# Moving the shared expert, the row buffers, the excess loop and the final additions of a mixture-of-experts kernel

## The chip, the cores and the metric

The kernel runs on 1 core of one Trainium2 chip. The metric is the device time of one execution in microseconds (us); lower is better. The median of the runs of the kernel before is 2158.79 us.

## The reference, cut to what matters

Two layers run one after the other. Each has a token mixer (attention and a gated spatial branch) and then a mixture of experts; the change lies in the second part alone. There are 512 tokens of width 1024 (`D`), 64 experts with an inner width of 256, and each token goes to 8 of them; one more expert, the shared one, sees every token.

```python
def run_block(args):
    e, toks, ws = args
    xb = x_pad[toks]
    hb = jax.nn.silu(xb @ w_gate[e]) * (xb @ w_up[e])
    return (hb @ w_down[e]) * ws[:, None]

yb = lax.map(run_block, (blk_expert, tok_buf.reshape(n_blocks, MOE_BLOCK), w_buf.reshape(n_blocks, MOE_BLOCK)))
routed = jax.ops.segment_sum(yb.reshape(P, D), tok_buf, num_segments=T + 1)[:T]
shared = (jax.nn.silu(xt @ ws_gate) * (xt @ ws_up)) @ ws_down
return (routed + shared).reshape(B, S, D)
```

The layer then adds this to `ALPHA * x` and normalises; the last layer also multiplies by a gain and adds a bias (`ln2_g`, `ln2_b`).

## The kernel before, in words

**Units.** `moe` sorts the experts by their number of tokens, at run time. The sorted experts have fixed capacities (`CAPS`), and these are cut into 43 units of 128 rows, u0 to u42; some hold part of a large expert, others two to four small ones. Which sorted expert lies in which unit is known when the program is built; only the expert's number is read at run time (`eid`). Each expert's weights are three loads of 1 MB: gate and up columns for one half of the inner sum, the same for the other half, and the down matrix. `load` (L787) issues them on SP.

**Ring of weight slots.** `wnew` hands out slots in turn: six (tag `w`) and three (tag `wd`), and after the routing two more (`w2`). The shared expert's three parts go through the same slots, and each is held until the last piece that reads it.

**One unit on PE.** `gate_up` (L800) runs half 0, then the h of the unit before is transposed (`turn`, L813), then `gate_up` half 1, and then `down` (L826) of the unit before. `scatter` (L1042, POOL) writes the unit's rows into the DRAM array `ysl`. Before each even unit PE transposes the token rows of a pair of units ahead (`turn_pair`, L1005), and `bring_pair` (L1021) works out the slots of the next pair and lets POOL gather its rows (L1026). The gathered rows stay in a row buffer until they are transposed.

**The shared expert** is cut into 12 pieces, three for each 128 tokens (half 0, half 1, and turn with down). `drain(side, n)` runs n of them: five while the routing is worked out, four at u0, two at u1 and one at u2. They read `hT`, a 16 KB per partition tile with the tag `L16`. The two row buffers for pairs from the third on (`rowbuf`) take the place of `hT`, so their gathers wait for the last gate and up piece.

**The loop for excess blocks** (`beyond`) serves experts with more rows than their capacity. It is a `For_i` over a count read at run time, in front of u14, with six weight parts already asked for (`AHEAD`). With these inputs the count is zero: the body never runs, but the engines meet at its branch.

**The end of a layer.** The last two units (`LATE = 2`) are not scattered: `late_mark` and `late` make one-hot matrices and split their rows, and L1266 adds them by matmuls. `collect` loads `ysl` back in 16 loads of 1 MB on SP (L1192), which go through the ring too. For each of the four 128-token tiles: eight matmuls of the late rows (L1266), four additions on DVE of half of the loaded slots (L1270), 16 identity matmuls for the other half (L1274), the sum into `x` (L1277), statistics and normalisation. In the last layer `affine` (L1256, L1257) applies `ln2_g` and `ln2_b`, which SP loads behind the 16 loads, into a ring slot.

**POOL's other work** is `stream`: three operations for each tile that fold `ln1_g`, `ln1_b` and the shared expert's rows into `x`; three steps of it run per unit from u3 on.

Of the kernel before, what the change touches and what calls it, by code (L numbers as in the profile page):

```python
# [41 lines left out]

BEYOND = 14
AHEAD = 6
assert len(CAPS) == E
# [129 lines left out]
def trunk(tc, A):  # L175
# [167 lines left out]
    def mixer(l, st):  # L343
# [352 lines left out]
        st["bring"] = bring  # L696
        t = bring.tile([128, 2048], F32, tag="w", bufs=6, name="rw")
        rw, rb = t[:, 0:NK * E].rearrange("p (k e) -> p k e", k=NK), t[:, NK * E:(NK + 1) * E]
# [53 lines left out]
    def moe(l, st):  # L752
# [12 lines left out]

        more = []
        turns = [0]

        def wnew():

            n = turns[0] % (9 + (MORE if more else 0))
            turns[0] += 1
            if n >= 9:
                return more[0].tile([128, 2048], F32, tag="w2", bufs=MORE, name="we")
            if n % 3 == 2:
                return bp.tile([128, 2048], F32, tag="wd", bufs=3, name="wd")
            return bring.tile([128, 2048], F32, tag="w", bufs=6, name="we")
# [61 lines left out]
        def shared():  # L839
            for i in range(NT):  # L840
                ps = psum()
                for half in range(2):
                    gate_up(hT[:, :, i * 128:(i + 1) * 128], SH, half, ps)
                    if half:
                        h = swiglu(ps, 128)
                    yield
                t = turn(h, 128)
                down(t, SH, 128, None, ysh[:, i])
                yield

# [211 lines left out]
        def bring_pair(p):  # L1062
# [4 lines left out]
            for b_, u_ in enumerate(units_of(p)):  # L1067
                G[u_] = slots(P, b_ * 128, UNITS[u_], None, rbuf[p % 2][:, b_])
                if u_ >= n_units - LATE:
                    zero = bp.tile([128, D], F32, tag="y", bufs=3, name="zero")  # L1070
                    gp.memset(zero, 0.0)
                    scatter(zero, G[u_][1])

        def turn_pair(p):
            xg = bp.tile([128, NK, 256], F32, tag="xg", bufs=2, name="xg")
            gather([rbuf[p % 2][:, b_] for b_ in range(len(units_of(p)))], xg)
            for b_, u_ in enumerate(units_of(p)):
# [3 lines left out]
        mark_pair(0)  # L1081
        rbuf[0] = bp.tile([128, 2, D], F32, tag="xg", bufs=2, name="rows")
        bring_pair(0)
        mark_pair(1)
        drain(side, 1)
        rbuf[1] = bp.tile([128, 2, D], F32, tag="xr", bufs=1, name="rows")
        bring_pair(1)
# [34 lines left out]
        off = small([128, 1], "off", keep=True)  # L1122
        turn_pair(0)
        got1 = rbuf[1]

        def beyond():

            free = rbuf[BEYOND // 2 % 2]
            nov = nc.values_load(ovr[0:1, 128:129], min_val=0, max_val=128)
# [24 lines left out]
        mark_pair(2)  # L1154
        more.append(ch)

        def stream():
            gp.tensor_scalar(lnr, lnr, ALPHA, None, op0=OP.mult)  # L1158
            for i in range(NT):
                gp.tensor_tensor(x[:, i], x[:, i], lnr[:, 0], op=OP.mult)  # L1160
                yield
                gp.tensor_tensor(x[:, i], x[:, i], lnr[:, 1], op=OP.add)
                yield
                gp.tensor_tensor(x[:, i], x[:, i], ysh[:, i], op=OP.add)
                yield

        slow = [stream()]
        lates = []
# [17 lines left out]
        def collect():  # L1186

            for i in range(NT):
                for a in range(TOP // 2):
# [3 lines left out]
                    got.append(t)  # L1193

        got = []
        for u_ in range(n_units + 1):
            if u_ % 2:
                mark_pair(u_ // 2 + 3)
            else:
                if u_ == BEYOND:  # L1200
                    for r, part in [(s[0], part) for u in UNITS[u_:] for part in range(3) for s in u][:AHEAD]:
                        get(r, part)
                    beyond()
                if u_ and units_of(u_ // 2 + 1):
# [3 lines left out]
            if u_ < n_units:  # L1208
                ps = psum()
                xT = G[u_][0]  # L1210
                gate_up(xT, UNITS[u_], 0, ps)
            if u_ >= 1:
# [4 lines left out]
            if u_ == 0:  # L1217
                rbuf[1] = got1
# [7 lines left out]
                gp.dma_start(lnr[:, 0], A["ln1_g"][l:l + 1, :].to_broadcast([128, D]))  # L1226
                gp.dma_start(lnr[:, 1], A["ln1_b"][l:l + 1, :].to_broadcast([128, D]))
            if u_ >= 1:
# [20 lines left out]
        if last:  # L1249
            lnr = bp.tile([128, 2, D], F32, tag="wd", bufs=3, name="lnr")  # L1250
            nc.sync.dma_start(lnr[:, 0], A["ln2_g"][l:l + 1, :].to_broadcast([128, D]))
            nc.sync.dma_start(lnr[:, 1], A["ln2_b"][l:l + 1, :].to_broadcast([128, D]))

        def affine(i):
            for eng, cs in ((dve, slice(0, 640)), (gp, slice(640, 1024))):
                eng.tensor_tensor(x[:, i, cs], x[:, i, cs], lnr[:, 0, cs], op=OP.mult)  # L1256
                eng.tensor_tensor(x[:, i, cs], x[:, i, cs], lnr[:, 1, cs], op=OP.add)  # L1257
            nc.sync.dma_start(A["out"][i * 128:(i + 1) * 128, :], x[:, i])

        for i in range(NT):  # L1260
            mine = got[i * TOP // 2:(i + 1) * TOP // 2]
            fin = [psum() for _ in range(2)]
            for n, (PT, yg) in enumerate(lates):
                for a in range(2):
                    for h in range(2):
                        pe.matmul(fin[h], PT[:, i * 128:(i + 1) * 128], yg[:, a, h * 512:(h + 1) * 512],  # L1266
                                  start=n == 0 and a == 0, stop=False)
            for t in mine[:2]:
                for j in range(2):
                    dve.tensor_tensor(x[:, i], x[:, i], t[:, j], op=OP.add)  # L1270
            for n, t in enumerate(mine[2:]):
# [156 lines left out]
```

## Time and profile before

| | us |
|---|---|
| runs of the kernel | 2158.79, 2152.85, 2159.09 |
| profiled execution | 2155.73 |
| its span in the trace | 2153.9 |
| PE busy | 1973.7 (92%) |
| DVE busy | 996.9 (46%) |
| ACT busy | 500.9 (23%) |
| POOL busy | 370.5 (17%) |

The profiled execution's own time is 1.8 us over its span and 3.1 us under the median. The page's 40 slices alternate between two kinds: the mixers, with little DMA, and the two expert stages (about 380 to 1075 us, and 1425 us to the end), where the 16 DMA engines move 350 to 420 GB/s in most slices while PE is nearly always busy too. A busy share of 92% on PE therefore doesn't tell which of the two sets the time inside an expert stage; the windows of a stage do.

### The profile page before, as it was taken

Reading aid. Unit: us, or ns where it says so; the run is one execution under the profiler, and the core shown is the slowest. Engines: PE = TensorE matmul, PEld = TensorE weight load, DVE = VectorE, ACT = ScalarE, POOL = GpSimd, SP = SyncE. Lnnn points to the kernel's source line nnn. Section 1 sums busy time; section 2 is a strip of 40 time slices with the busy share of each in tenths; the row PEclk is TensorE's granted clock in tenths of the full one; section 3 lists DMA queues with packets and bytes.
Section 4 is the critical chain, followed back from the end, with each engine's and each line's share of the span. In section 5 each row is a group of like instructions: output and inputs, shape, how many; then the busy total and the mean of one; then the engine's idle time right before and its main releaser. Section 6 shows DMA issues by size and latency. Waiting matters only on the chain. (4 is left out here: it accounts for less than half of the span.)

```text
span 2153.9 us, 29150 instructions
## 1 busy us (share of the span) xinstructions
PE 1973.7 (92%) x10820; PEld 1105.5 (51%) x10820; DVE 996.9 (46%) x2065; ACT 500.9 (23%) x1015; POOL 370.5 (17%) x355
## 2 busy tenths in 40 slices
PE   5999999889979999999999999989899799999993
PEld 4867788443334433333477688864433344333341
DVE  6767867523323332321668575753243233332245
ACT  3474232211111111111155533221111111111110
POOL 1101101015411111111130000010361111111113
PEclk9999999899999999999999999989999999999997
DMA  7503665558989999998853144545799899999983
GB/s 277 184 31 134 212 213 186 216 190 355 420 366 407 421 420 402 412 416 373 348 184 108 37 151 165 182 173 204 269 408 415 359 422 420 415 411 415 405 350 157
DMA packets 120128, 626.29 MB, mean 291 GB/s; under 512 B 19472, under 2 KB 19472, under 8 KB 65968
## 3 DMA queue, kind: packets, MB, share of 16 engines
q1 hardware_dynamic: 92912, 550.99, 64.8%
q0 software_dynamic: 27072, 73.42, 9.2%
q8 instruction: 86, 1.41, 0.3%
q14 instruction: 58, 0.48, 0.1%
HBM read 596.02 MB, written 51.38 MB: 301 GB/s over the span
## 5 line engine op out<-in xcount | busy, mean ns | idle before, releaser
L800 PE MATMUL ps<-we,xg 128*32 128x512 f32 (+2 forms) x2544 | 573.0, 597 | 10.2 <-DMA we<-in_w_exp 10.1
L826 PE MATMUL ps<-we,hTt 128*32 128x512 f32 (+2 forms) x1344 | 315.1, 599 | 15.3 <-DMA we<-in_w_exp 11.5
L807 DVE TENSOR_TENSOR h<-h,ps 128x256 f32<-128x256 f32 x94 | 39.6, 421 | 574.0 <-ACT h L805 574.0
L800 PEld LDWEIGHTS ps<-we,xg 128*32 128x32 f32 (+2 forms) x2544 | 171.4, 124 | 254.2 <-issue 210.2
L800 PE MATMUL ps<-wd,xg 128*32 128x512 f32 (+2 forms) x1104 | 286.4, 601 | 3.5 <-DMA wd<-in_w_exp 3.5
L832 DVE SCALAR_TENSOR_TENSOR y<-ps,wc,r 128x512 f32<-128x512 f32 x172 | 129.1, 751 | 197.8 <-PE ps L826 197.8
L1042 POOL DMA_INDIRECT ysl<-y,ii x82 | 85.9, 1047 | 729.0 <-DVE y L832 626.5
L298 PE MATMUL ps<-wH,hH 128*128 128x512 f32 (+1 forms) x512 | 196.2, 383 | 4.2 <-ACT hH L193 4.2
L299 PE MATMUL ps<-wL,hH 128*128 128x512 f32 (+1 forms) x512 | 194.2, 379 | 1.5 <-DVE wL L295 1.5
L300 PE MATMUL ps<-wH,hL 128*128 128x512 f32 (+1 forms) x512 | 194.1, 379 | 0.0
L826 PEld LDWEIGHTS ps<-we,hTt 128*32 128x32 f32 (+2 forms) x1344 | 96.0, 124 | 172.3 <-issue 131.5
L826 PE MATMUL ps<-wd,hTt 128*32 128x512 f32 (+2 forms) x544 | 166.5, 608 | 12.8 <-DMA wd<-in_w_exp 6.8
L1012 ACT ACTIVATE xg<-ps,f 128x256 f32<-128x256 f32 (+1 forms) x176 | 85.4, 556 | 241.4 <-DVE xg L1014 241.4
L193 ACT ACTIVATE hTt<-ps 128x256 f32<-128x256 f32 x94 | 36.0, 383 | 453.5 <-PE ps L813 453.3
L193 ACT ACTIVATE wH<-w 128x1024 fp32r<-128x1024 f32 x83 | 87.6, 1059 | 196.3 <-PE ps L300 110.6
L800 PEld LDWEIGHTS ps<-wd,xg 128*32 128x32 f32 (+2 forms) x1104 | 79.3, 123 | 101.7 <-issue 87.3
L295 DVE TENSOR_TENSOR wL<-w,wH 128x1024 fp32r<-128x1024 f32 x84 | 102.3, 1220 | 50.0 <-ACT wH L193 50.0
L805 ACT ACTIVATE h<-ps 128x256 f32<-128x256 f32 x94 | 36.0, 383 | 357.5 <-PE ps L800 357.5
L1005 PE MATMUL ps<-kc,rowbuf 128*128 128x128 f32 x624 | 83.9, 290 | 37.6 <-DMA we<-in_w_exp 21.9
L1026 POOL DMA_INDIRECT rowbuf<-xd,it x78 | 79.6, 1021 | 221.8 <-PE ps L800 104.6
L236 DVE SCALAR_TENSOR_TENSOR acc<-wa,cond,acc 128x1024 f32<-128x1024 f32 x80 | 106.5, 1331 | 7.5 <-DMA acc<-in_b_ada 4.0
L298 PEld LDWEIGHTS ps<-wH,hH 128*128 128x128 f32 x512 | 97.5, 190 | 23.2 <-ACT hH L193 5.3
(330 smaller groups left out, 2703.3 us busy)
## 6 DMA issues: line engine op xcount, KB each, us to landing
we<-in_w_exp SPq DMA_DIRECT2D x280, 1024.0 KB, 21.4
wd<-in_w_exp SPq DMA_DIRECT2D x104, 1024.0 KB, 20.9
wa<-in_w_ada SPq DMA_DIRECT2D x96, 512.0 KB, 4.4
w<-in_wA SPq DMA_DIRECT2D x92, 512.0 KB, 4.4
we<-ysl SPq DMA_DIRECT2D x24, 1024.0 KB, 18.0
wd<-ysl SPq DMA_DIRECT2D x8, 1024.0 KB, 17.9
we<-in_w_sh SPq DMA_DIRECT2D x4, 1024.0 KB, 9.8
xd<-x SPq DMA_DIRECT2D x8, 512.0 KB, 4.1
```

The costliest lines, as they stand in the source:

```text
L193: return act.activation(out, in_, AF.Copy)
L236: dve.scalar_tensor_tensor(acc, w, cond[:, k:k + 1], acc, op0=OP.mult, op1=OP.add)
L295: dve.tensor_sub(l_out, src, h_out.bitcast(F32))
L298: pe.matmul(ps, aH, wH, start=first, stop=False)
L299: pe.matmul(ps, aH, wL, start=False, stop=False)
L300: pe.matmul(ps, aL, wH, start=False, stop=last)
L800: pe.matmul(ps[c:c + m, :], xT[:, k, c:c + m], ws[s][:, kk * 512:(kk + 1) * 512], start=k == 0, stop=k == NK - 1)
L826: pe.matmul(ps[c:c + m, :], t[:, j, c:c + m], ws[s][:, j * 1024 + nh * 512:j * 1024 + (nh + 1) * 512], start=j == 0, stop=j == 1)
L832: dve.scalar_tensor_tensor(y[0:n, hs], ps[0:n], wcol[0:n], gate2[0:n, hs], op0=OP.mult, op1=OP.mult)
L1005: pe.transpose(ps[:, kk * 256 + b_ * 128:kk * 256 + (b_ + 1) * 128], r[:, (k2 * 2 + kk) * 128:(k2 * 2 + kk + 1) * 128], ident)
L1012: act.activation(xg[:, k, 0:n], o, AF.Identity, bias=sh2[:, k:k + 1], scale=sc2[:, k:k + 1])
L1042: gp.indirect_dma_start(out=ysl[l], out_offset=IndirectOffsetOnAxis(ap=ii[:, 0:1], axis=0), in_=y, in_offset=None, bounds_check=T * TOP - ...
```

## The change

1. **Own slots for the shared expert.** Its three parts get slots `s`, `s`, `sd`. The experts' ring is `w, w, wd` twice, with the two `w2` eight slots; when the last shared piece is done, `s`, `sd`, `s` join it (eleven).
2. **The 12 pieces** are spread: three in the routing, then one at each unit from u3 to u11 (`SIDE = 3`); the call at u12 ends the generator, which extends the ring, loads `ln1_g` and `ln1_b` (POOL's queue) and starts `stream`.
3. `turn_pair(0)` and u0's half 0 stand between the steps of the routing where two shared pieces stood.
4. **One row buffer** (tag `xr`, two units) in place of two; a pair's rows are transposed before the next pair is gathered.
5. **`beyond()`** stands at u41, behind the last weight loads and ahead of `collect`, without loads ahead of its own.
6. **The additions of tiles 0 and 1** (`add`, L1210) are issued at u42, those of tiles 2 and 3 in their tile as before.
7. `ln2_g` and `ln2_b` are loaded on POOL's queue into the row buffer's place.

PE at the end of the routing, layer 0: `we,hT` are gate and up matmuls of the shared expert, `we,xg` of a unit; L1097 to L1113 are the routing's last steps. Before:

```order
L1021 MATMUL ps<-WT,P 128x196 x8
L800 MATMUL ps<-we,hT 128x512 x4
L1097 MATMUL ps<-ov,kc 64x1
L1098 MATMUL ps<-ones,ov 1x1
L800 MATMUL ps<-we,hT 128x512 x4
L1112 MATMUL ps<-le,ones 1x128
L1113 MATMUL ps<-lt,capb 128x128
L1005 MATMUL ps<-kc,rows 128x128 x16
L800 MATMUL ps<-we,xg 32x512 x16
```

And now (L1028 is the transpose, L1044 the slots):

```order
L1044 MATMUL ps<-WT,P 128x196 x8
L1028 MATMUL ps<-kc,rows 128x128 x16
L1120 MATMUL ps<-ov,kc 64x1
L1121 MATMUL ps<-ones,ov 1x1
L800 MATMUL ps<-we,xg 32x512 x16
L1136 MATMUL ps<-le,ones 1x128
L1137 MATMUL ps<-lt,capb 128x128
L800 MATMUL ps<-wd,xg 32x512 x3
```

The two shared pieces are gone from here, and u0's half 0 stands in the chain, with its second half right behind.

PE near the layer's end, now: u41's second half, u40's down, the loop with its body, then u42.

```order
L800 MATMUL ps<-we,xg 128x512 x4
L826 MATMUL ps<-we,hTt 128x512 x4
L1151 TENSOR_LOAD ovr
L1152 COMPARE_AND_BRANCH
L1152 UNCONDITIONAL_BRANCH x2
...
L1152 UNCONDITIONAL_BRANCH
L800 MATMUL ps<-wd,xg 128x512 x4
L813 MATMUL ps<-kc,h 128x128 x2
L800 MATMUL ps<-we,xg 128x512 x4
L826 MATMUL ps<-we,hTt 128x512 x4
L813 MATMUL ps<-kc,h 128x128 x2
L826 MATMUL ps<-we,hTt 128x512 x4
L1276 MATMUL ps<-yg,PT 128x512 x8
```

The branch, which stood between u13's half 1 with u12's down and u14's half 0, now lies between u40's down and u42's half 0.

DVE at the same place; `ix` and `PT` are the one-hot matrix of a late unit, `y` its rows, `yg` their split. Before:

```order
L295 TENSOR_TENSOR yg<-y,yg 128x512 x2
L1173 TENSOR_SCALAR ix<-tk 128x1
L1174 TENSOR_SCALAR PT<-kc,tk 128x256
L1175 TENSOR_SCALAR PT<-kc,ix 128x256
L832 SCALAR_TENSOR_TENSOR y<-ps,wc,r_2302 128x512 x2
L295 TENSOR_TENSOR yg<-y,yg 128x512 x2
L1270 TENSOR_TENSOR x<-x,we 128x1024 x4
L1277 TENSOR_TENSOR x<-ps,x 128x512 x2
```

And now (with the tiles' numbers, which tell u41's from u42's):

```order
L294 TENSOR_TENSOR yg_8283<-y_8274,yg_8283 128x512 x2
L1210 TENSOR_TENSOR x_69<-x_69,we_8219 128x1024 x2
L1210 TENSOR_TENSOR x_69<-x_69,wd_8221 128x1024 x2
L1210 TENSOR_TENSOR x_69<-x_69,we_8227 128x1024 x2
L1210 TENSOR_TENSOR x_69<-x_69,wd_8229 128x1024 x2
L1185 TENSOR_SCALAR ix_8302<-tk_7745 128x1
L1186 TENSOR_SCALAR PT_8301<-kc_65,tk_7745 128x256
L1187 TENSOR_SCALAR PT_8301<-kc_65,ix_8302 128x256
L832 SCALAR_TENSOR_TENSOR y_8306<-ps_8307,wc_7743,r5_2302 128x512
L294 TENSOR_TENSOR yg_8315<-y_8306,yg_8315 128x512 x2
L1286 TENSOR_TENSOR x_69<-ps_8320,x_69 128x512
```

Eight additions, of tiles 0 and 1, now stand between the split of u41's rows and everything that u42's rows need.

```diff
-BEYOND = 14
-AHEAD = 6
+SIDE = 3
...
-        more = []
+        ring = ["w", "w", "wd"] * 2
         turns = [0]
...
+        from_pool = {"w": (bring, 4), "wd": (bp, 2), "s": (bring, 2), "sd": (bp, 1)}
+
+        def wnew(tag=None):
+
+            if tag is None:
+                tag = ring[turns[0] % len(ring)]
+                turns[0] += 1
+            p, n = from_pool[tag]
+            return p.tile([128, 2048], F32, tag=tag, bufs=n, name="wd" if tag in ("wd", "sd") else "we")
 
         def load(which, part):
-            t = wnew()
+            t = wnew(("s", "s", "sd")[part] if which == "shared" else None)
...
                 down(t, SH, 128, None, ysh[:, i])
+                yield
+
+            ring.extend(["s", "sd", "s"])
+            gp.dma_start(lnr()[:, 0], A["ln1_g"][l:l + 1, :].to_broadcast([128, D]))
+            gp.dma_start(lnr()[:, 1], A["ln1_b"][l:l + 1, :].to_broadcast([128, D]))
+            slow.append(stream())
...
-                G[u_] = slots(P, b_ * 128, UNITS[u_], None, rbuf[p % 2][:, b_])
+                if b_ == 0:
+                    rbuf[p] = bp.tile([128, 2, D], F32, tag="xr" if p else "xg", bufs=1 if p else 2, name="rows")
+                G[u_] = slots(P, b_ * 128, UNITS[u_], None, rbuf[p][:, b_])
...
-        drain(side, 1)
+        turn_pair(0)
...
-        drain(side, 1)
+        ps0 = psum()
+        gate_up(G[0][0], UNITS[0], 0, ps0)
...
-        turn_pair(0)
-        got1 = rbuf[1]
...
-        more.append(ch)
...
+        from_pool["w2"] = ch, MORE
+        ring.extend(["w2"] * MORE)
+
...
+        def add(i):
+            for t in got[i * TOP // 2:i * TOP // 2 + 2]:
+                for j in range(2):
+                    dve.tensor_tensor(x[:, i], x[:, i], t[:, j], op=OP.add)
+
...
-                if u_ == BEYOND:
-                    for r, part in [(s[0], part) for u in UNITS[u_:] for part in range(3) for s in u][:AHEAD]:
-                        get(r, part)
-                    beyond()
...
-                lnr = bp.tile([128, 2, D], F32, tag="xr", bufs=1, name="lnr")
-                drain(side, 4)
-
-                rowbuf = bring.tile([128, 4, D], F32, tag="L16", name="rowbuf")
-                rbuf[0], rbuf[1] = rowbuf[:, 0:2], rowbuf[:, 2:4]
                 bring_pair(2)
...
+                    beyond()
                     collect()
-                drain(side, 2)
-                if u_ > 2:
+                if u_ == n_units - 1:
+                    add(0)
+                    add(1)
+                if u_ >= SIDE:
                     drain(slow, 3)
+                    drain(side, 1)
...
-            lnr = bp.tile([128, 2, D], F32, tag="wd", bufs=3, name="lnr")
-            nc.sync.dma_start(lnr[:, 0], A["ln2_g"][l:l + 1, :].to_broadcast([128, D]))
-            nc.sync.dma_start(lnr[:, 1], A["ln2_b"][l:l + 1, :].to_broadcast([128, D]))
+            last_ln = bp.tile([128, 2, D], F32, tag="xr", bufs=1, name="lnr")
+            gp.dma_start(last_ln[:, 0], A["ln2_g"][l:l + 1, :].to_broadcast([128, D]))
+            gp.dma_start(last_ln[:, 1], A["ln2_b"][l:l + 1, :].to_broadcast([128, D]))
...
-            for t in mine[:2]:
-                for j in range(2):
-                    dve.tensor_tensor(x[:, i], x[:, i], t[:, j], op=OP.add)
+            if i > 1:
+                add(i)
```

## Rows read from the trace of the kernel before

**Rows 1.** Windows, layer 0: bounds, length, busy by engine, PE's clock, DMA share, GB/s

```profile
430.00:440.00 10.00, 8.44 (x39) 4.71 (x33) 3.61 (x7) 2.59 (x6) 0.00 (x0) 1.00 0.87 365
440.00:450.00 10.00, 8.54 (x22) 3.54 (x20) 1.11 (x2) 0.77 (x2) 0.00 (x0) 1.00 0.00 0
450.00:460.00 10.00, 10.00 (x91) 3.59 (x93) 3.47 (x16) 1.44 (x4) 0.00 (x0) 1.00 0.39 148
460.00:470.00 10.00, 9.17 (x36) 3.35 (x28) 1.88 (x3) 0.38 (x1) 0.56 (x1) 1.00 0.69 273
470.00:480.00 10.00, 4.95 (x25) 4.69 (x26) 2.22 (x5) 2.12 (x4) 3.61 (x5) 0.66 0.71 216
480.00:490.00 10.00, 10.00 (x47) 3.90 (x50) 2.41 (x14) 1.35 (x5) 2.08 (x2) 1.00 0.31 92
490.00:500.00 10.00, 9.53 (x60) 3.07 (x56) 3.40 (x6) 0.77 (x2) 1.01 (x1) 1.00 0.79 287
500.00:600.00 100.00, 99.25 (x522) 40.41 (x516) 35.66 (x102) 15.64 (x40) 50.58 (x29) 1.00 1.01 414
630.00:640.00 10.00, 1.91 (x5) 0.57 (x3) 1.50 (x2) 0.00 (x0) 0.98 (x1) 0.82 0.79 328
640.00:650.00 10.00, 7.13 (x36) 5.39 (x38) 3.17 (x14) 2.70 (x6) 1.28 (x2) 0.67 0.63 247
```

**Rows 2.** Timeline of PE, layer 0, u0 to u12: start, length, instructions, [idle before]

```profile
423.37 3.64 PE L800 MATMUL ps<-we,xg 128*32 128x512 f32 x32
437.66 7.03 PE L800 MATMUL ps<-we,hT 128*128 128x512 f32 x16
474.02 0.45 PE L1005 MATMUL ps<-kc,rowbuf 128*128 128x128 f32 x1 [4.85 <-DMA rowbuf<-xd,it]
475.49 3.46 PE L1005 MATMUL ps<-kc,rowbuf 128*128 128x128 f32 x15 [1.03 <-DMA rowbuf<-xd,it]
...
607.23 1.97 PE L1005 MATMUL ps<-kc,rowbuf 128*128 128x128 f32 x16
...
609.91 3.62 PE L800 MATMUL ps<-we,xg 128*128 128x512 f32 x8
```

**Rows 3.** Timeline of PE at the loop in front of u14, layers 0 and 1

```profile
628.21 3.70 PE L826 MATMUL ps<-we,hTt 128*128 128x512 f32 x8
642.87 3.68 PE L1005 MATMUL ps<-kc,rowbuf 128*128 128x128 f32 x16 [10.96 <-DMA we<-in_w_exp]
...
1687.22 3.04 PE L1005 MATMUL ps<-kc,rowbuf 128*128 128x128 f32 x13 [10.90 <-DMA we<-in_w_exp]
```

**Rows 4.** Timeline of PE at the end of layer 0, from u40's down on

```profile
1019.07 3.60 PE L826 MATMUL ps<-we,hTt 128*128 128x512 f32 x8
1022.50 3.60 PE L800 MATMUL ps<-wd,xg 128*128 128x512 f32 x8
...
1041.23 3.59 PE L1274 MATMUL ps<-wd,kc 128*128 128x512 f32 x8
...
1068.58 7.13 PE L1274 MATMUL ps<-we,kc 128*128 128x512 f32 x16 [0.98 <-DMA we<-ysl]
```

**Rows 5.** Timeline of DVE at the end of layer 0

```profile
1033.89 1.47 DVE L295 TENSOR_TENSOR yg<-y,yg 128x512 fp32r<-128x512 f32 x2
...
1036.98 0.75 DVE L832 SCALAR_TENSOR_TENSOR y<-ps,wc,r 128x512 f32<-128x512 f32 x1 [1.03 <-PE ps L826]
...
1040.76 5.00 DVE L1270 TENSOR_TENSOR x<-x,we 128x1024 f32<-128x1024 f32 x4
1047.44 0.69 DVE L1277 TENSOR_TENSOR x<-ps,x 128x512 f32<-128x512 f32 x1 [1.68 <-PE ps L1274]
```

**Rows 6.** The chain that ended last, end of layer 1: start, length, what

```profile
2066.33 4.95 DMA ysl<-y,ii
...
2099.87 17.39 DMA lnr<-in_ln_b
...
2134.99 1.29 DVE x L1277 x2
```

More of the change, by code (lines that the diff above doesn't have):

```diff
@@ L696, in mixer @@
         st["bring"] = bring
-        t = bring.tile([128, 2048], F32, tag="w", bufs=6, name="rw")
+        t = bring.tile([128, 2048], F32, tag="w", bufs=4, name="rw")
         rw, rb = t[:, 0:NK * E].rearrange("p (k e) -> p k e", k=NK), t[:, NK * E:(NK + 1) * E]
@@ L764, in moe @@
         eid = bp.tile([1, E], I32, name="eid")
-        more = []
+        ring = ["w", "w", "wd"] * 2
         turns = [0]
[L769 to L777, printed above, removed]
+        from_pool = {"w": (bring, 4), "wd": (bp, 2), "s": (bring, 2), "sd": (bp, 1)}
[5 more added lines that the diff above has]
+            return p.tile([128, 2048], F32, tag=tag, bufs=n, name="wd" if tag in ("wd", "sd") else "we")
         def load(which, part):
-            t = wnew()
+            t = wnew(("s", "s", "sd")[part] if which == "shared" else None)
             if which == "shared":
@@ L848, in shared, with lnr, stream @@
                 down(t, SH, 128, None, ysh[:, i])
+                yield
[3 more added lines that the diff above has]
+            slow.append(stream())
+        keep = {}
+        slow = []
+        def lnr():
+            if "lnr" not in keep:
+                keep["lnr"] = bring.tile([128, 2, D], F32, tag="L16", name="lnr")
+            return keep["lnr"]
+        def stream():
+            gp.tensor_scalar(lnr(), lnr(), ALPHA, None, op0=OP.mult)
+            for i in range(NT):
+                gp.tensor_tensor(x[:, i], x[:, i], lnr()[:, 0], op=OP.mult)
+                yield
+                gp.tensor_tensor(x[:, i], x[:, i], lnr()[:, 1], op=OP.add)
+                yield
+                gp.tensor_tensor(x[:, i], x[:, i], ysh[:, i], op=OP.add)
                 yield
@@ L1075, in turn_pair @@
             xg = bp.tile([128, NK, 256], F32, tag="xg", bufs=2, name="xg")
-            gather([rbuf[p % 2][:, b_] for b_ in range(len(units_of(p)))], xg)
+            gather([rbuf[p][:, b_] for b_ in range(len(units_of(p)))], xg)
             for b_, u_ in enumerate(units_of(p)):
@@ L1081, in moe @@
         mark_pair(0)
-        rbuf[0] = bp.tile([128, 2, D], F32, tag="xg", bufs=2, name="rows")
         bring_pair(0)
@@ L1085, in moe @@
         drain(side, 1)
-        rbuf[1] = bp.tile([128, 2, D], F32, tag="xr", bufs=1, name="rows")
         bring_pair(1)
@@ L1122, in moe @@
         off = small([128, 1], "off", keep=True)
-        turn_pair(0)
-        got1 = rbuf[1]
         def beyond():
-            free = rbuf[BEYOND // 2 % 2]
+            free = bp.tile([128, 2, D], F32, tag="xr", bufs=1, name="rows")
             nov = nc.values_load(ovr[0:1, 128:129], min_val=0, max_val=128)
@@ L1154, in moe @@
         mark_pair(2)
-        more.append(ch)
[L1157 to L1167, printed above, removed]
+        from_pool["w2"] = ch, MORE
+        ring.extend(["w2"] * MORE)
         lates = []
@@ L1208, in moe @@
             if u_ < n_units:
-                ps = psum()
+                ps = psum() if u_ else ps0
                 xT = G[u_][0]
-                gate_up(xT, UNITS[u_], 0, ps)
+                if u_:
+                    gate_up(xT, UNITS[u_], 0, ps)
             if u_ >= 1:
@@ L1241, in moe @@
                                 get(r, part)
+                    beyond()
                     collect()
-                drain(side, 2)
-                if u_ > 2:
+                if u_ == n_units - 1:
+                    add(0)
+                    add(1)
+                if u_ >= SIDE:
                     drain(slow, 3)
+                    drain(side, 1)
         last = l == DEPTH - 1
         if last:
-            lnr = bp.tile([128, 2, D], F32, tag="wd", bufs=3, name="lnr")
-            nc.sync.dma_start(lnr[:, 0], A["ln2_g"][l:l + 1, :].to_broadcast([128, D]))
-            nc.sync.dma_start(lnr[:, 1], A["ln2_b"][l:l + 1, :].to_broadcast([128, D]))
+            last_ln = bp.tile([128, 2, D], F32, tag="xr", bufs=1, name="lnr")
+            gp.dma_start(last_ln[:, 0], A["ln2_g"][l:l + 1, :].to_broadcast([128, D]))
+            gp.dma_start(last_ln[:, 1], A["ln2_b"][l:l + 1, :].to_broadcast([128, D]))
         def affine(i):
             for eng, cs in ((dve, slice(0, 640)), (gp, slice(640, 1024))):
-                eng.tensor_tensor(x[:, i, cs], x[:, i, cs], lnr[:, 0, cs], op=OP.mult)
-                eng.tensor_tensor(x[:, i, cs], x[:, i, cs], lnr[:, 1, cs], op=OP.add)
+                eng.tensor_tensor(x[:, i, cs], x[:, i, cs], last_ln[:, 0, cs], op=OP.mult)
+                eng.tensor_tensor(x[:, i, cs], x[:, i, cs], last_ln[:, 1, cs], op=OP.add)
             nc.sync.dma_start(A["out"][i * 128:(i + 1) * 128, :], x[:, i])
```

3 lines of the change are left out of this document (removed).

## The prediction

> **What bounds the kernel now.** I read the windows of layer 0's expert stage first, then PE's timeline where the windows change character, then DVE and the chain at the end of each layer. Layer 1's stage has the same units in the same order, so layer 0 stands for both; its loop waits 10.90 us against 10.96 [rows 3].
>
> From 500 us on the DMA share is 1.01 [rows 1]: transfers bound the long middle of the stage, and PE, busy 99%, only just keeps up. Between 430 and 500 us the reader sees the opposite: shares of 0.87, 0.00, 0.39, 0.69, 0.71, 0.31 and 0.79. The shortfalls add up to 32.4 us in which transfers did nothing, while PE worked on shared pieces and on u0 to u3. PE lost far less there: 10 minus busy over the seven windows gives 9.4 us, most of it at 474 us, where the transposes wait for gathered rows [rows 2]. At the loop the windows show DMA shares of 0.79 and 0.63, 5.8 us lost, and PE idle 10.96 us [rows 1, 3]. The end of a layer is bound by PE and its feeding: from u40's down on, PE runs almost without a gap to 1075.7 us [rows 4], 53.0 us after that down's end at 1022.67. In layer 1 DVE is held by the row of `ln2_b`, which lands at 2117.26 [rows 6].
>
> **Part 1: shared pieces, ring, row buffer, u0's early half, and the loop gone from u14.** The work is unchanged, only moved. PE from u0's first matmul to u12's takes 609.91 - 423.37 = 186.5 us [rows 2]. Of that 9.4 + 0.75 us are idle [rows 1], and the 15 transposes at 475.49 take 3.46 us where 16 take 1.97 elsewhere: they ran at half the clock, 1.6 us more [rows 2]. That leaves 174.8 us of work. The two pieces taken out of the routing (7.0 us by the pair at 437.66 [rows 2]) now follow u0, so the stretch needs 181.8 us; but u0 starts up to those 7.0 us sooner. At its best PE thus reaches u12 by 9.4 + 0.75 + 1.6 = 11.7 us sooner. The loop's 5.8 us of lost transfers come on top, 17.5 us: the far bound of gain. The near bound is 0, if the smaller ring takes all of it.
>
> What decides between them is how long transfers still stand idle. Units u0 to u11 hold 18 experts: 54 loads of 1.05 MB and 24 moves of rows of 0.52 MB, together 69 MB, at 414 GB/s [rows 1] 167 us. PE needs 182. So in this stretch **PE sets the pace in the changed kernel**, and transfers lose 15 us there whatever the slots are. At 2.5 us a load eight slots fill in 20 us, and u0's last slot comes free only with its down at the end of u1, some 30 us after the first load: 10 us more. Three slots join only at u12, 7.5 us of loads that can't run ahead. 15 + 10 + 7.5 = 32.5 us against 32.4 + 5.8 = 38.2 now. I take **6 us gained per layer**. That is nearer the near bound, because of the slots: a unit with two whole experts takes six of the eight.
>
> The single row buffer costs nothing: a pair's transposes stand ahead of the next pair's slots on PE, and the gather has two units, 25 us, until it is used. If that cover went, the price would be the 4.85 us wait at 474 us [rows 2]. `stream` on POOL starts ten units later and still ends long before its result is used.
>
> **Part 2: the loop at u41.** All engines meet there with every transfer landed, u40's scatter too. At u14 the same branch held PE for 10.96 us, with preloaded weights in flight [rows 3]. At the end the weights have landed, and a scatter takes 4.95 us from issue [rows 6]; about 1 us for `y` and the issue ahead of it and 1 us for the branch behind make 7 us. Bounds: 5 and 11. PE then starts again at half clock: 16 transposes after the loop took 3.68 us for 1.97, and the window's granted clock was 0.67 [rows 1, 3]. I take 2 us. What waits behind is all of u42 and the final matmuls. `collect` loses little: before, SP had to wait for the same scatter.
> The Trainium skill (Advanced Engine Details and Errata, Control Flow Timing) puts a compare-and-branch at about 108 ns; with that as the whole price the sum below would be 9 us lower in each layer, 2150, but the 10.96 us of this trace speak against it, since what costs is the meeting and not the branch.
>
> **Part 3: eight additions ahead of u42's rows.** DVE works in order. One addition takes 5.00 / 4 = 1.25 us [rows 5], eight 10.0 us, and they now stand between the split of u41's rows and u42's `PT`, `y` and `yg`. Before, DVE had 1.03 us of slack there [rows 5]. So `yg` of u42 comes 9 us later, and PE's late matmuls of tile 0 wait for it. PE idle that long starts at half clock once more: 2 us. The additions taken from tiles 0 and 1 give nothing back: at 1047.44 DVE had finished its four and waited 1.68 us for PE [rows 5], and a tile needs 8.7 us of PE (34.5 us for four [rows 4]) but less on DVE: 5.00 + 2 x 0.69 = 6.4 us and two short statistics. Bounds: 0, if something else holds PE as long, and 12.
> Layer 0's end: 7 + 2 + 9 + 2 = **+20 us**.
>
> **Part 4: layer 1's end.** Here the same delay meets a hidden wait. u40's scatter starts at 2066.33, so its down ended about 2065.3; 53.0 us later, at 2118.3, the last sum into `x` would have stood if PE alone decided. It stood at 2134.99 [rows 6], because `affine` waited for `ln2_b`. With those rows loaded early that wait of 16.7 us is gone, and what is late next is PE: 2118.3 + 20 = 2138.3, that is +3.3, and `affine` on DVE adds under 1. **+4 us**.
>
> **Sum.** -6 - 6 + 20 + 4 = +12 us on the profiled execution's 2155.73 us: **2168 us**. That execution lies 3.1 us under the median of 2158.79, so the forecast is +0.4% against the median. About 0.3%, 6.5 us, is what a measurement of this kernel can tell from no change: slower means above 2165.3, faster below 2152.3.
>
> **The rivals.**
> *The idle transfers come back.* If transfers, not PE, set the pace of u0 to u11, most of the 32.4 + 5.8 us returns, with only the first 12 or so lost: 26 us per layer, 2155.7 - 52 + 24 = **2128**. For it: the empty window at 440 us [rows 1]. Against it: PE's 182 us against 167.
> The Trainium skill (Perfetto Trace Analysis, Optimization Strategy) says that stages with different most-contended engines may gain from being interleaved, which is what this does to the pieces; the rule would give this rival's time, and rows 1 bear out its premise, but not that PE has room.
> *PE's account in full.* The far bound of part 1, 17.5 us per layer: -35 + 24, **2145**. It holds if u0 starts the whole 7 us sooner and no unit waits for a slot.
> *A draw.* 12 us per layer, PE's gain alone, equal to the end's loss: **2156**.
> *The ring of eight starves PE* (slower still). A two-expert unit wants six loads, 15 us, in about 12.4 us of PE; u6, u7, u10, u11 are such, and with eight slots the lead built up in u2 to u5 is two loads. If each pair costs its shortfall of 2 x 2.6 us, and the three joining slots no less, PE loses about 12 where it gained 6: +6 per layer, **2192**. It decides if PE in u6 to u11 waits for weights for over 12 us in all.
>
> **How the numbers follow.** The forecast has 0.42, the idle transfers 0.12, PE's account in full 0.14, the draw 0.20, the starving ring 0.12. Faster: 0.12 + 0.14 = 0.26. Same: the draw and 0.03 from the forecast's lower edge, 0.23. Slower: 0.51. The range, 2143 to 2186, leaves out the first rival and half of the last; the forecast's own is 2160 to 2180.
>
> **What would show it.** Part 1 is right if the windows from 430 to 600 us show PE nearly always busy with DMA well under 1, and u12 starts 4 to 8 us sooner; wrong if DMA is at 1.0 from 440 us on. Part 2: an idle PE of 5 to 11 us between u40's down and u42's half 0. Part 3: PE waiting for `yg` some 9 us ahead of tile 0's late matmuls, with eight additions on DVE in that time. Part 4: no wait for `ln2_b` in the chain, and the last sum about 73 us after u40's down. The forecast falls if DVE's additions wait for loads instead (the end is then longer still), or if u12 is over 12 us sooner.

## The result, and the profile of the changed kernel

The changed kernel takes 2167.08 us (median of five runs, 2164.55 to 2176.26; a sixth took 2172.42). The kernel before took 2153.5 us in the same session. The ratio is 1.0064, 95% interval 1.0037 to 1.0091: **slower by 0.6%**. Forecast were 2168 us and "slower". The profiled execution is the slowest of the five, 2176.26 us with a span of 2174.5, so its stages are compared one by one below, and its whole only with care.

The end of layer 0 first. PE's timeline of the changed kernel, against [rows 4] (start, length, instructions, [idle before]; L1276 are the late rows' matmuls, L1283 the identity matmuls):

```profile
1020.53 3.60 PE L826 MATMUL ps<-we,hTt 128*128 128x512 f32 x8
1030.47 6.01 PE L800 MATMUL ps<-wd,xg 128*128 128x512 f32 x8 [6.34 <-issue]
...
1048.48 1.50 PE L1276 MATMUL ps<-yg,PT 128*128 128x512 f32 x4
1057.54 2.31 PE L1276 MATMUL ps<-yg,PT 128*128 128x512 f32 x4 [7.56 <-ACT yg L192]
1059.64 8.44 PE L1283 MATMUL ps<-we,kc 128*128 128x512 f32 x16
...
1087.18 7.03 PE L1283 MATMUL ps<-we,kc 128*128 128x512 f32 x16
```

Two new gaps are to be seen, 6.34 us at the loop and 7.56 us ahead of the late rows of u42, and behind each a group that runs slowly: eight matmuls in 6.01 us, which took 3.60 before, and sixteen in 8.44, which take 7.03 further on. PE's granted clock (the figure before the DMA share) is below 1.00 in the windows of both groups:

```profile
1030.00:1040.00 10.00, 9.53 (x19) 4.27 (x20) 0.00 (x0) 0.38 (x1) 0.00 (x0) 0.74 0.92 365
1050.00:1060.00 10.00, 2.46 (x5) 1.75 (x6) 8.72 (x12) 1.26 (x2) 0.00 (x0) 0.61 1.00 397
```

DVE in the same stretch, against [rows 5], shows what stood in the way the second time:

```profile
1044.27 1.47 DVE L294 TENSOR_TENSOR yg<-y,yg 128x512 fp32r<-128x512 f32 x2
1045.66 2.48 DVE L1210 TENSOR_TENSOR x<-x,we 128x1024 f32<-128x1024 f32 x2
...
1053.09 2.48 DVE L1210 TENSOR_TENSOR x<-x,wd 128x1024 f32<-128x1024 f32 x2
...
1056.07 1.40 DVE L832 SCALAR_TENSOR_TENSOR y<-ps,wc,r 128x512 f32<-128x512 f32 x2
1057.52 1.35 DVE L294 TENSOR_TENSOR yg<-y,yg 128x512 fp32r<-128x512 f32 x2
```

DVE never stands still from 1044.27 to 1055.5: the additions are not waiting for loads, they are simply in front. The chain of layer 1's end, against [rows 6] (start, length, what), runs over the same places and no longer over `ln2_b`:

```profile
2080.89 4.82 DMA ysl<-y,ii
2085.71 1.42 issue
2087.12 6.75 PE ps L800 x8
...
2114.93 2.31 PE ps L1276 x4
2117.24 8.60 PE ps L1283 x16
...
2155.35 1.29 DVE x L1286 x2
```

The windows of layer 0's stage, against [rows 1] (bounds, length, busy by engine, PE's granted clock, DMA share, GB/s):

```profile
410.00:420.00 10.00, 6.90 (x20) 3.24 (x20) 4.23 (x21) 0.67 (x2) 3.38 (x4) 0.80 0.85 336
420.00:430.00 10.00, 10.00 (x79) 4.33 (x81) 5.21 (x17) 2.15 (x4) 0.00 (x0) 0.83 0.30 97
430.00:440.00 10.00, 10.00 (x90) 4.61 (x86) 4.56 (x19) 3.15 (x8) 2.02 (x2) 1.00 1.02 430
440.00:450.00 10.00, 6.40 (x55) 2.61 (x48) 2.15 (x4) 0.38 (x1) 1.01 (x1) 0.90 1.02 417
450.00:460.00 10.00, 10.00 (x34) 6.71 (x33) 3.27 (x16) 3.20 (x7) 2.03 (x2) 0.76 1.01 419
...
490.00:500.00 10.00, 10.00 (x52) 3.15 (x44) 3.53 (x8) 0.38 (x1) 1.01 (x1) 1.00 0.60 207
500.00:600.00 100.00, 97.73 (x446) 40.36 (x444) 28.29 (x82) 13.26 (x34) 12.33 (x12) 1.00 0.84 324
...
620.00:630.00 10.00, 10.00 (x66) 2.89 (x68) 3.19 (x6) 0.77 (x2) 2.37 (x3) 1.00 0.42 162
```

The empty stretch from 440 to 500 us is filled, but transfers now stand idle elsewhere: 7 us from 420 to 430, 8.5 from 460 to 500, 16 from 500 to 600 and 5.8 at u12. PE is the busy one in all these windows. From 410 to 650 us transfers stand idle for 39.9 us in all; before it was 43.3.

For all kernels I took five times from PE's timeline. The **stage** runs from the first slots matmul to the start of u40's down (before: 403.77 to 1019.07 in layer 0), the **wait part** from there to the first late matmul, the **final part** to the last identity matmul's end, and in layer 1 the rest to the span's end. Layers 0 and 1 stand side by side; the median and the ratio are of the runs.

| kernel | stage | wait part | final part | rest | median us | ratio to before |
|---|---|---|---|---|---|---|
| before | 615.3, 616.3 | 19.0, 19.3 | 37.6, 38.5 | 34.5 | 2153.5 to 2156.9 | |
| changed | 613.9, 611.0 | 28.0, 29.6 | 45.7, 46.1 | 22.6 | 2167.08 | 1.0064 (1.0037 to 1.0091) |
| changed, additions in tiles | 607.9, 611.2 | 27.6, 28.1 | 36.3, 36.3 | 22.5 | 2151.2 | 0.9973 (0.9964 to 0.9982) |
| changed, loop at u14 | 622.1, 619.6 | 19.0, 19.3 | 48.9, 51.7 | 22.5 | 2182.45 | 1.0115 (1.0100 to 1.0130) |
| both of these | 619.4, 623.7 | 19.0, 19.1 | 37.9, 39.7 | 20.5 | 2157.11 | 0.9995 (0.9985 to 1.0005) |
| before, early ln2 rows | 616.8, 616.2 | 19.0, 19.0 | 37.6, 39.7 | 20.2 | 2147.35 | 0.9948 (0.9933 to 0.9963) |
| before, no loop | 608.7, 608.6 | 19.0, 19.2 | 37.3, 37.9 | 34.5 | 2145.44 | 0.9952 (0.9936 to 0.9968) |
| additions in tiles, pieces early | 606.8, 605.4 | 28.6, 28.8 | 36.3, 36.3 | 22.4 | 2142.28 | 0.9928 (0.9913 to 0.9943) |
| before, loop at u2, early ln2 | 614.1, 610.8 | 19.0, 19.3 | 37.5, 39.9 | 20.1 | 2137.87 | 0.9921 (0.9904 to 0.9939) |
| before, loop inside u2, early ln2 | 610.3, 613.1 | 19.0, 19.2 | 37.9, 39.8 | 20.1 | 2135.68 | 0.9911 (0.9896 to 0.9926) |
| pieces early, loop inside u2 | 621.2, 621.8 | 19.0, 19.0 | 37.9, 39.0 | 19.9 | 2156.72 | 1.0005 (0.9994 to 1.0015) |
| before, one row buffer | 614.8, 618.7 | 19.0, 19.0 | 37.9, 38.2 | 34.5 | 2154.52 | 0.9995 (0.9983 to 1.0007) |

One stage is one execution. Where the same code was profiled twice the two differ by up to 6 us (613.9 and 607.9 in the second and third rows: their stages have the same code), so a stage is used only where both layers and the median agree.

From before to changed, the two stages gain 1.4 + 5.3 = 6.7 us, layer 0's end loses 73.7 - 56.6 = 17.1, layer 1's 98.3 - 92.3 = 6.0: +16.4. The mixers, which the change doesn't touch, were 4.2 us slower in this execution; together that is the 20.6 us between the spans. With the stages of the third row, which have the same code, the two would gain 7.4 + 5.1 = 12.5 us in place of 6.7.

### The profile page after: what moved, and what is told of

Same layout as the page of the kernel before. It is cut to its first block, busy times and chain, and to the rows that moved or that the text cites. A ratio compares the mean times of both kernels' runs of the same rounds, so it can differ in the third digit from the quotient of the medians.

```text
span 2174.5 us, 29113 instructions
## 1 busy us (share of the span) xinstructions
PE 1996.8 (92%) x10820; PEld 1116.2 (51%) x10820; DVE 1009.8 (46%) x2065; ACT 499.9 (23%) x1015; POOL 371.5 (17%) x357
## 5 line engine op out<-in xcount | busy, mean ns | idle before, releaser
L800 PE MATMUL ps<-we,xg 128*32 128x512 f32 (+2 forms) x2544 | 557.4, 604 | 15.6 <-DMA we<-in_w_exp 15.5
L826 PE MATMUL ps<-we,hTt 128*32 128x512 f32 (+2 forms) x1376 | 328.5, 598 | 28.2 <-DMA we<-in_w_exp 25.1
L800 PE MATMUL ps<-wd,xg 128*32 128x512 f32 (+2 forms) x1104 | 298.4, 602 | 17.5 <-issue 13.6
L800 PEld LDWEIGHTS ps<-we,xg 128*32 128x32 f32 (+2 forms) x2544 | 164.7, 123 | 248.5 <-issue 196.3
L826 PEld LDWEIGHTS ps<-we,hTt 128*32 128x32 f32 (+2 forms) x1376 | 101.2, 126 | 217.2 <-issue 158.0
L800 PEld LDWEIGHTS ps<-wd,xg 128*32 128x32 f32 (+2 forms) x1104 | 87.7, 128 | 131.8 <-issue 112.3
L826 PE MATMUL ps<-wd,hTt 128*32 128x512 f32 (+2 forms) x512 | 139.4, 608 | 3.8 <-ACT hTt L192 3.8
L1049 POOL DMA_INDIRECT rows<-xd,it x86 | 88.4, 1028 | 233.5 <-issue 117.8
L298 PEld LDWEIGHTS ps<-wL,hH 128*128 128x128 f32 x512 | 97.7, 191 | 21.4 <-DVE wL L294 3.6
## 6 DMA issues: line engine op xcount, KB each, us to landing
we<-in_w_exp SPq DMA_DIRECT2D x282, 1024.0 KB, 20.2
```

Of the source, the lines that this page charges most:

```text
L298: pe.matmul(ps, aH, wL, start=False, stop=False)
L800: pe.matmul(ps[c:c + m, :], xT[:, k, c:c + m], ws[s][:, kk * 512:(kk + 1) * 512], start=k == 0, stop=k == NK - 1)
L826: pe.matmul(ps[c:c + m, :], t[:, j, c:c + m], ws[s][:, j * 1024 + nh * 512:j * 1024 + (nh + 1) * 512], start=j == 0, stop=j == 1)
L1049: gp.indirect_dma_start(out=row, out_offset=None, in_=xd, in_offset=IndirectOffsetOnAxis(ap=it[:, 0:1], axis=0), bounds_check=T - 1, oob_i ...
```

## The experiments

**The additions of tiles 0 and 1 back in their tiles.**

```diff
-                if u_ == n_units - 1:
-                    add(0)
-                    add(1)
...
-            if i > 1:
-                add(i)
+            add(i)
```

> The changed kernel with the additions of tiles 0 and 1 back in their tiles; all else as changed. Theory (part 3 of the prediction): the eight additions held u42's rows 7.6 us in layer 0's trace and cost a start at half clock; without them layer 0's end is 8 to 10 us shorter and layer 1's 4 to 8, about 2152. Rival (the loop's wait alone lengthens the end and the additions lie in its shadow): within 3 us of the changed kernel, 2164 to 2170.

Measured 2151.2 us, 16 under the changed kernel by the medians and some 20 by the ratios (0.9973 against 1.0064). The final part falls from 45.7 and 46.1 to 36.3 in both layers, and PE's timeline has the late matmuls together again, in layer 0:

```profile
1041.46 1.72 PE L1273 MATMUL ps<-yg,PT 128*128 128x512 f32 x5
1043.53 1.23 PE L1273 MATMUL ps<-yg,PT 128*128 128x512 f32 x3 [0.35 <-ACT yg L192]
1044.59 7.03 PE L1279 MATMUL ps<-we,kc 128*128 128x512 f32 x16
```

The theory holds in both layers: about 9.5 us each for calls that stood one unit too early. Layer 1, at 9.8, lies over the 4 to 8 that were expected there. This edit alone turns the change from 0.6% slower to 0.3% faster than before.

**The loop back at u14.**

```diff
+                if u_ == 14:
+                    for r, part in [(s[0], part) for u in UNITS[u_:] for part in range(3) for s in u][:6]:
+                        get(r, part)
+                    beyond()
...
-                    beyond()
                     collect()
```

> The changed kernel with the loop for excess blocks back in front of u14's slots, six loads asked for ahead of it; all else as changed. Theory (part 2): each end gets about 9 us shorter (7 of waiting, 2 of half clock), and the stage loses again the 5.8 us of transfers per layer, so -3 per layer, about 2161. Rival (in the stage the loop costs nothing, because the transfers wait for PE there anyway): -9 per layer, about 2149. Second rival (the changed ring has less lead, so the meeting costs more than before): 2167 or over.

Measured 2182.45 us, over the changed kernel. The wait part is 19 us again, as expected, but the final part, with its additions, grows to 48.9 and 51.7 (in layer 0 PE waits 10.28 us for `yg`: it arrives sooner, and one of the additions ahead waits 2.58 us for its load) and the stage to 622 and 620. The theory falls on its price for the meeting at u14; the time is the second rival's.

**Both edits together**, by the two diffs above.

> The edits of the first two runs together: what is left of the change is the shared expert's slots, the spread pieces, u0's early half, the single row buffer and the early ln2 rows. Theory: the two parts of the end add up, -15 and -6, about 2146; against the kernel before with early ln2 rows this shows the early part alone, within 4 us of it. Rival (spreading the pieces gains by itself once nothing else is paid): 10 us or more under that kernel.

Measured 2157.11, the kernel before to within a tenth of a per cent, and 10 us over the one with only early ln2 rows: neither the theory nor the rival. What the loop waited for is in this kernel's timelines, PE first and then POOL (layer 0):

```profile
643.58 2.03 PE L1044 MATMUL ps<-WT,P 128*128 128x196 f32 x8 [13.80 <-POOL x L871]
```

```profile
630.20 5.39 POOL L865 TENSOR_SCALAR lnr<-lnr 128x2048 f32<-128x2048 f32 x1
...
640.51 2.34 POOL L871 TENSOR_TENSOR x<-x,ysh 128x1024 f32<-128x1024 f32 x1
```

The changed order starts `stream` at u13. A loop at u14 then waits for POOL's folding as well, 13.80 us where it was 10.96 [rows 3]; in layer 1 PE waited 14.75 us, and a weight load came last. So the spread pieces and the loop's place hang together: with the loop left at u14 the spread order, with its slots, is 10 us slower than the old one.

**The kernel before with early ln2 rows.**

```diff
-            lnr = bp.tile([128, 2, D], F32, tag="wd", bufs=3, name="lnr")
-            nc.sync.dma_start(lnr[:, 0], A["ln2_g"][l:l + 1, :].to_broadcast([128, D]))
-            nc.sync.dma_start(lnr[:, 1], A["ln2_b"][l:l + 1, :].to_broadcast([128, D]))
+            lnr = bp.tile([128, 2, D], F32, tag="xr", bufs=1, name="lnr")
+            gp.dma_start(lnr[:, 0], A["ln2_g"][l:l + 1, :].to_broadcast([128, D]))
+            gp.dma_start(lnr[:, 1], A["ln2_b"][l:l + 1, :].to_broadcast([128, D]))
```

> The kernel before with one edit: ln2_g and ln2_b are loaded on POOL's queue into the row tile of ln1, which is done by then, and not on SP behind the 16 loads. Theory (part 4): the wait for ln2_b ends layer 1 up to 16.7 us late; without it DVE's own work in affine (about 10.7 us a tile in the changed kernel's chain, against 8.7 of PE) is the next bound, so -10 to -16 us, 2138 to 2144. Rival (DVE's work is the bound anyway and the wait lies beside it): less than 4 us gained, over 2149.

Measured 2147.35, 9.4 under before: just beside the theory's range. The rest after PE's end falls from 34.5 to 20.2 us. The last sum into `x` stands 56.2 us after the end of u40's down, where it was 69.7: 13.5 of the 16.7 us came back. The rest is DVE's, which takes 10.7 us a tile in the chain, from one `x` L1277 to the next.

```profile
2115.94 1.29 DVE x L1277 x2
...
2126.66 1.29 DVE x L1277 x2
```

That was so in the kernel before as well, from this line of its chain to the last one in [rows 6], 2134.99:

```profile
2124.28 1.29 DVE x L1277 x2
```

Why the medians fell by 9.4 us and not by 13 isn't shown; in this execution the mixers took 3.8 us longer than in that of the kernel before.

**The kernel before without the loop.** The loop for excess blocks is left out.

```diff
                         get(r, part)
-                    beyond()
```

> The kernel before without the loop for excess blocks: that part of the computation is left out (with these inputs its count is zero). All else as before, the six loads asked for ahead too. This measures the loop's price at u14 by itself. In the traces so far the expert stage (first slots matmul to u40's down) takes 615 to 617 us before, 608 to 614 with the changed ring and no loop in it, 619 to 624 with the changed ring and the loop back at u14. Theory (ring and spread pieces are worth nothing by themselves, only the loop's removal gains): the stage here comes to 608 to 611, about -6 per layer, 2145. Rival (the changed ring pays by itself): the stage stays at 613 or more, so under 3 us per layer gained. Second rival (the changed ring of eight costs): the stage falls under 606, over 10 us per layer gained.

Measured 2145.44, and a stage of 608.7 and 608.6: the loop cost 6.6 and 7.7 us per layer at u14. The changed kernel's stage without a loop in it is 607.9 to 613.9. So the changed stage gained no more than the loop's removal gives by itself; taken together, the spread pieces and their ring gained nothing.

**The shared pieces early again**, in the kernel with the additions in their tiles.

```diff
                 turn_pair(1)
+                drain(side, 4)
                 bring_pair(2)
...
+                drain(side, 3)
                 if u_ >= SIDE:
                     drain(slow, 3)
-                    drain(side, 1)
```

> The changed kernel with the additions in their tiles, and with the shared pieces back at four in u0, three in u1 and two in u2, so that the shared expert's slots join the ring at u2 and not at u12. Loop at u41, own slots, one row buffer and early ln2 rows as changed. Theory (PE sets the pace in u0 to u11, the work is only moved): the stage stays within 4 us of the same kernel with spread pieces (608 and 611 us), about 2151. Rival (spreading the pieces is what pays): transfers stand idle from 440 to 500 us as before and the stage is 10 us or more longer per layer, over 2170. Second rival (the late joining of the three slots costs): the stage is 5 or more shorter, under 2142.

Measured 2142.28, 9 us under the spread pieces: at the edge of the second rival. The stage is 606.8 and 605.4, with transfers idle early as before. Its windows in layer 0:

```profile
470.00:480.00 10.00, 10.00 (x44) 5.96 (x43) 3.88 (x17) 2.44 (x7) 1.98 (x2) 1.00 0.05 11
480.00:490.00 10.00, 10.00 (x48) 3.51 (x46) 1.93 (x3) 0.71 (x2) 1.06 (x2) 1.00 0.44 142
490.00:500.00 10.00, 8.48 (x46) 2.77 (x44) 3.07 (x6) 0.77 (x2) 1.16 (x2) 1.00 0.99 386
500.00:600.00 100.00, 97.88 (x517) 40.04 (x518) 35.73 (x102) 15.68 (x40) 51.06 (x29) 1.00 0.99 402
```

The transfers are nearly empty at 470 us, much as before at 440, and from 490 on, with eleven slots, they are full, where the same kernel with spread pieces shows a share of 0.91 from 500 to 600. The gain lies behind u12. From the first slots matmul to u12's transposes this kernel takes 203.4 and 200.4 us, the same one with spread pieces 198.6 and 202.0; from there to u40's down it takes 403.4 and 405.0 against 409.3 and 409.2. SP's wait table of the changed kernel from 605 to 640 us shows a cause at u12:

```profile
SPq L787 <- PE ps L800: 22.5, 1, 22.5
```

For 22.5 us SP stood in front of a load until PE's gate and up matmuls freed a slot (22.5 too with the additions in their tiles); with early pieces its longest wait for a slot from 600 to 640 is 6.8. The late joining of the three slots is thus seen to cost transfers. How much of the 9 us it is stays open, since the same edit also brings `stream` forward.

**The kernel before with the loop at u2**, and early ln2 rows.

```diff
-BEYOND = 14
+BEYOND = 2
...
-                drain(side, 2)
+                drain(side, 3)
```

> The kernel before with the ln2 rows loaded early, as in the run of that edit, and with the loop at u2 in place of u14 (the last shared piece moves from u2 to u1 for it). There PE waits for the gathered rows anyway and the transfers stand idle, so the meeting should cost little. Theory: the loop's price at u14 comes back, less 1 to 3 us at u2: the stage falls from 616 to 608 to 612 us in each layer, about 2147 - 12 = 2135, the fastest so far. Rival (the meeting holds PE where PE sets the pace, so it costs as much as at u14): 2145 to 2150.

Measured 2137.87: near the theory in time, but the stage kept 614.1 and 610.8. PE waited 9.53 us at the loop. The wait table of SP's queue from 460 to 490 us shows for what (us in total, times, longest):

```profile
SPq L1130 <- DMA lnr<-in_ln_g: 22.1, 1, 22.1
SPq L1130 <- DMA ysl<-y,ii: 1.9, 1, 1.9
SPq L1130 <- DMA lnr<-in_ln_b: 1.4, 1, 1.4
```

The three waits follow one another. SP stood at the loop from 458.3 us on; POOL issued `ln1_g` and `ln1_b` only at 472.6 and 473.2, and u0's scatter at 474.07; PE came to the branch at 476.15. The rows landed at 480.4 and 481.8, the scatter last, at 483.8. So the scatter ended the meeting, and SP had stood there 25 us in all; whether it would have landed sooner without the rows ahead of it on POOL's queue isn't shown.

**The loop inside u2**, in the kernel before with early ln2 rows.

```diff
...
+            if u_ == BEYOND:
+                for r in dict.fromkeys(s[0] for s in UNITS[u_ - 1]):
+                    get(r, 2)
+                for r in dict.fromkeys(s[0] for u in UNITS[u_:u_ + 2] for s in u):
+                    for part in range(3):
+                        get(r, part)
+                beyond()
+                bring_pair(u_ // 2 + 2)
...
```

The call at the unit's start goes; the other lines are those of the run before.

> The kernel before with early ln2 rows, the last shared piece in u1, and the loop inside u2: between u2's half 1 and u1's down, with the slots of pair 3 behind it; u1's and u2's missing loads and u3's are asked for ahead of it. At u2's start the loop still cost 2 to 5 us per layer, because u0's scatter had just been issued; inside the unit that scatter has landed and the ring is full. Theory (what costs is the landing of the last scatter and the start at half clock behind it): the stage falls to 609 to 611 us in both layers, about 2134. Rival (the branch itself or what is asked for ahead of it costs as much): the stage stays at 611 to 614 or over, 2138 or more.

Measured 2135.68, the fastest, 0.9% under before. PE's wait at the loop shrinks to this:

```profile
487.73 1.14 PE L1021 MATMUL ps<-WT,P 128*128 128x196 f32 x8 [2.42 <-SPq L785]
```

The stage is 610.3 in layer 0, as the theory expected, and 613.1 in layer 1, as the rival did; against the run at u2's start the gain of 2 us is within what the two intervals allow.

**The same place in the kernel with early pieces**, and with the ring of eight.

```diff
-                drain(side, 3)
+                drain(side, 5)
...
+            if u_ == BEYOND:
+                for r in dict.fromkeys(s[0] for s in UNITS[u_ - 1]):
+                    get(r, 2)
+                for r in dict.fromkeys(s[0] for s in UNITS[u_]):
+                    get(r, 2)
+                beyond()
+                bring_pair(u_ // 2 + 2)
...
-                    beyond()
                     collect()
```

> The changed kernel with the additions in their tiles, the shared pieces early (four in u0, five in u1) and the loop inside u2, between its half 1 and u1's down, with the slots of pair 3 behind it. Against the run with the pieces early and the loop at u41, the end loses 28.7 - 19 = 9 us per layer of waiting and half clock, and gives back 1.3, since the 16 loads are then less far ahead of PE. Theory: the stage stays at 606 to 609, so about -12 to -16, 2127 to 2131, the fastest. Rival (with a ring of eight at that point the meeting drains what little lead there is): the stage comes to 612 or more, 2138 or over.

Measured 2156.72: the rival. SP came to the loop long before the others. Its wait table from 400 to 560 us and the windows show it:

```profile
SPq L1153 <- DVEq L1153: 24.6, 1, 24.6
```

```profile
470.00:480.00 10.00, 8.60 (x22) 3.54 (x20) 1.05 (x2) 0.77 (x2) 0.00 (x0) 1.00 0.00 0
480.00:490.00 10.00, 10.00 (x38) 5.49 (x37) 3.19 (x6) 2.32 (x5) 0.00 (x0) 1.00 0.00 0
```

SP stood at the loop for 8.8 us until the scatter landed and then for 24.6 until DVE came, and in two windows of 10 us nothing was moved. Not all of that is the loop's: without it, in the run with early pieces above, these windows show shares of 0.05 and 0.44 and the next one 0.99, where it is 0.51 here. From 470 to 500 us transfers so stood idle for 24.9 us against 15.2. PE itself waited only 2.35 us at the branch. A meeting costs twice: PE's wait, and the loads that the queue standing at it doesn't issue.

**One row buffer in the kernel before.**

```diff
-                rbuf[0], rbuf[1] = rowbuf[:, 0:2], rowbuf[:, 2:4]
+                rbuf[0], rbuf[1], spare[0] = rowbuf[:, 0:2], rowbuf[:, 0:2], rowbuf[:, 2:4]
```

> The kernel before with one row buffer: every pair from the third on uses the first half of the tile that held two, the loop's body the other half; pieces, ring, loop and end as before. In the changed kernel's trace PE waited 3.60 us for pair 2's rows and ran at half clock behind it, in the stretch in which the prediction put the single buffer at nothing. Theory of the prediction (a pair's rows are transposed before the next gather and are needed 25 us later): the stage stays at 615 to 617 us, 2154 to 2158. Rival (the gather, late by the transposes ahead of it, is waited for): the stage is 3 us or more longer per layer, over 2162.

Measured 2154.52 against 2155.72: the prediction's reading. Two row buffers in the changed kernel weren't tried.

## Why the prediction was right, point by point

**What bounds the stage.** Shown. "PE sets the pace in the changed kernel" in u0 to u11: its windows have PE at 10 of 10 while transfers idle. The idle transfers came out as worked: about 10 us at the start were forecast, 8.5 are in the windows from 410 to 430 (5.1 of such idle time stood there before as well, which the prediction didn't count); 15 in the PE-bound stretch, 16 from 500 to 600 and 8.5 from 460 to 500; 7.5 at u12, 6.9 from 620 to 640. They weren't removed, only spread. The rival "the idle transfers come back" fell by this.

**Part 1's size.** Not settled. -12 us for both layers were forecast; -6.7 were measured in the changed kernel's profile, which is its slowest run, and -12.5 in the profile with the additions in tiles, whose stages have the same code. The loop's removal alone is worth 6.6 + 7.7 = 14.3. The sign to look for was u12 starting 4 to 8 us sooner. Its transposes start 203.5 and 206.3 us after the first slots matmul before (layers 0 and 1), 204.8 and 201.4 in the changed kernel, 198.6 and 202.0 with the additions in tiles: once 1.3 us later, three times 4.3 to 4.9 sooner. From there to u40's down it is 411.8 and 410.0 before, 409.1 to 409.6 in all four changed stages, and 405.4 and 405.9 in the kernel before without the loop. So the mean gain of 4.8 us a layer is near the 6 forecast. But of the 5 us that the loop's removal gives behind u12 the changed kernel loses 3.7 again; the likely place is at u12, with the slots that join late, whose 7.5 us of idle transfers the prediction had counted. The shared expert's own slots and u0's early half weren't tried by themselves.

In layer 0 of the changed kernel PE also waited in two places that I had left out: for pair 0's rows, which the two shared pieces in the routing used to cover, and for pair 2's:

```profile
417.86 0.33 PE L1028 MATMUL ps<-kc,rows 128*128 128x128 f32 x1 [1.59 <-DMA rows<-xd,it]
...
448.83 3.46 PE L1028 MATMUL ps<-kc,rows 128*128 128x128 f32 x15 [3.60 <-DMA rows<-xd,it]
```

Behind the second it ran at half clock, 3.46 us for 15, with a granted clock of 0.76 in the window, as before at 474 [rows 2]: the same kind of wait, at another time. That the single buffer costs nothing in steady running was right; that pair 2's rows would be there, with the stage starting so much sooner and the weights filling the transfers, I had not worked out. They don't explain the one late u12: in layer 1 the same waits were 1.85 and 2.77 us, and its u12 came 4.9 us sooner. Why it was late stays open; single stages scatter by up to 6 us.

**Part 2.** Right in mechanism and size: 7 us of waiting and 2 at half clock forecast, 6.34 and 7.30 us of waiting measured, and 6.01 and 6.75 us for a group of 3.6. The wait part grew by 9.0 and 10.3. The Trainium skill's figure of about 108 ns for a compare-and-branch (Advanced Engine Details and Errata, Control Flow Timing) is no price for a loop's entry here: what is paid is the landing of the last scatter, 4.82 us in the chain, and 1.42 behind it.

**Part 3.** Right: 9 + 2 forecast per layer; 7.56 and 7.57 us of waiting and a final part of +8.1 and +7.6 measured, 9.4 and 9.8 against the run without the early additions.

**Part 4.** +4 forecast, +6.0 measured. The wait for `ln2_b` is gone, as read. "`affine` on DVE adds under 1" was too small: in the chain DVE takes 10.7 us a tile, more than PE's 8.7, so the last sum stands 75.5 us after u40's down and not 73. The 10.7 us could have been read from the trace of before, where it is the same (2124.28 to 2134.99): the 6.4 us that the prediction gave DVE for a tile come from layer 0, which has no `affine`.

**The sum.** +12 was forecast; the parts of the traces add up to +16.4, and the medians differ by 13.6. The stages of this profile gained 5 us less than forecast, layer 0's end lost 3 less, layer 1's 2 more. That 2167.08 lies within 1 us of 2168 is in part luck: these errors offset one another, and the forecast started from 2155.73, where the median of the kernel before came to 2153.5.

## What to carry to other kernels

In an engine's in-order queue a call belongs behind whatever the busiest engine waits for next: eight additions that nothing was waiting for cost 9.5 us per layer, because they were issued one unit too early. Put a loop whose body seldom runs where its queues have nothing in flight and nothing to issue, and look at the DMA queues that meet there, not only at the engines. Filling an idle resource gains nothing while another one sets the pace; the idle time only moves.

## What the hardware showed that was not expected

A loop's entry holds SP's queue for as long as its slowest party: 24.6 us for DVE in one run, during which two windows of 10 us moved 0 GB/s; in another SP stood 25 us, and the transfers on POOL's queue, two broadcast rows and a scatter, landed last. The same empty loop held PE for 2.03 to 14.75 us, by where it stood and what was in flight: 6.34 and 7.30 at u41, 10.96 and 10.90 at u14 before.
